# A hybrid transformer layer: the head's convolution from PSUM, wide squares, q's norms by a ones column, decay differences on GpSimd

## The chip, the cores and the metric

The kernel runs on one core of one Trainium2 chip. The metric is the time of one execution in microseconds; each kernel is run three times and the median counts. One further execution is recorded by the hardware profiler, and all rows below come from it. Names of engines: PE is TensorE (matmuls; PEld its weight loads), DVE is VectorE, ACT is ScalarE, POOL is GpSimd, SP is SyncE, which issues the transfers.

## What is computed

One layer on 512 latent and 256 context tokens, 1024 channels wide: a gated feed-forward half step, a mixing step, a second half step, a norm. The mixing step projects the normalised input with one large matrix. Eight heads of 128 channels each take q, k and v from it; this is the part that the change touches. The reference, cut to it:

```python
def short_conv(x, w):                     # 5 taps along the tokens, centred, per channel
    pad = CONV_K // 2
    xp = jnp.pad(x, ((0, 0), (pad, pad), (0, 0)))
    y = sum(xp[:, k:k + L] * w[k] for k in range(CONV_K))
    return jax.nn.silu(y)

def l2norm(x):
    return x * lax.rsqrt(jnp.sum(x * x, axis=-1, keepdims=True) + EPS)
...
    q = l2norm(q) * GDN_HEAD_DIM ** -0.5
    k = l2norm(k)
...
    diff = cum[..., :, None] - cum[..., None, :]      # inside a chunk
    decay = jnp.where(incl, jnp.exp(jnp.where(incl, diff, 0.0)), 0.0)
    lmat = jnp.where(strict, jnp.einsum('nbhid,nbhjd->nbhij', kb, kc) * decay, 0.0)
    sol = lax.linalg.triangular_solve(lmat + eye, rhs, lower=True, unit_diagonal=True)
...
    o = rmsnorm(o.astype(dt), gdn_norm_w) * jax.nn.silu(gate)
```

Every chunk of tokens gives a triangular system, whose inverse feeds a scan over the chunks, once forward and once backward. Context tokens need only k and v.

## The kernel before

Channels lie on the 128 partitions and tokens along the free axis; the kernel works with six chunks of 128 tokens (four latent, two context). Each projection (`job`, L132) is the sum of three matmuls for each of eight slices of the inner dimension, with weights and activations split into a high and a low half; its result for the latent tokens fills one PSUM bank of 512 columns, that for the context tokens (256) another. PSUM has eight banks in three rings: four with tag "b", which the jobs use, two "g" for the scan and two "a" for norms and inversion.

The heads' stage is a software pipeline. `front` makes k's transposed copy kt and the norms of q and k for one head, `invert` builds and inverts the triangular blocks of the head before it, `scan` runs the head before that, and `head` projects and convolves q, k and v of the head three ahead. These are generators; a string of letters gives the order in which their steps are issued, and a list scheduler with its own costs then orders the instructions of each engine. Each engine works through its row in that order.

The steps around the change:

- `conv_silu` (L567 to L587): ACT copies the job's result from PSUM to the padded tile raw (L575, L580), and scales it by the middle tap into cv (L576, L581); DVE adds the four other taps, 772 columns wide for k and v and 512 for q (L583); ACT's silu writes kf, qf or vf (L585, L587). raw and cv exist once each. POOL clears their paddings (L573, L574, L578, L579).
- `front`: k is transposed on PE (L764), ACT copies it to kt (L765) and squares each of the six chunks with an accumulated sum (L768, one read of the accumulator behind each); q is transposed (L771) and squared in the same way (L774). DVE adds epsilon (L776, L777), POOL raises to a power (rr, L780).
- `invert`: rows of cumulated decay come by transfer into crow; ACT makes the absolute difference to each of the twelve columns (arg, L817) and the exponential (L819); DVE multiplies it into L (L827) and into aqk (L836); POOL masks aqk (affine select, L838) and clears ti (L855, L856). ACT copies the diagonal blocks to din (L848), DVE transposes them to au (L850). Then the forward substitution: fifteen steps, each a product tm (L866) and a sum into ti (L868), both on DVE, and two transposes of ti (L870, L872). PE's products that complete the inverse follow (L881 to L926), with copies on ACT and the last products into L on DVE (L930, L934).
- `scan`: for each chunk products on PE (L952, L963, L973, L985, L997), and between them R (L956), vw (L976), S (L994) and ot (L999) on DVE, vn (L980) and scalings on ACT. At its end ACT squares the output in four pieces (L1007), DVE writes y (L1016).
- Weights of the heads' projections are split by ACT (whi, L119) and POOL (wlo, L120); those of the gates by ACT and DVE.

The lines that set this order:

```python
ORDER = "sfifsisiissiis"
for k in range(-2, H):
    stages = {c: g(i) for c, g, i in (("s", scan, k), ("f", front, k + 2), ("i", invert, k + 1)) if 0 <= i < H}
    for c in ORDER:
        if c in stages:
            next(stages[c], None)
```

Of the kernel before, what the change touches and what calls it, by code (L numbers as in the profile page):

```python
# [18 lines left out]
LAT = 512  # L19
# [5 lines left out]
EPS = 1e-6  # L25
# [6 lines left out]
PARTS = {"lat": (0, LAT), "ctx": (LAT, CTX)}  # L32
# [9 lines left out]
def layer_kernel(ctx, tc, a, out):  # L42
    nc = tc.nc
    act, dve, pool, pe, sp = nc.scalar, nc.vector, nc.gpsimd, nc.tensor, nc.sync
# [512 lines left out]
    def bc(ap, shape):  # L557
        return ap.to_broadcast(shape)
# [6 lines left out]
    kf, qf, vf = {}, {}, {}  # L565

    def conv_silu(w, tl, parts, dst, r=None):  # L567
        r = r or job(w, u_hi, u_lo, range(KT), parts)
        raw = pj.tile([128, 776], F32, tag="raw", name="raw", bufs=1)
        cv = pj.tile([128, 772], F32, tag="cv", name="cv", bufs=1)  # L570
        n = 772 if len(parts) == 2 else 512
        tap = [vec[:, 1, 24 * t + tl:24 * t + tl + 1] for t in range(5)]
        pool.memset(raw[:, 0:2], 0.0)  # L573
        pool.memset(raw[:, 514:518], 0.0)  # L574
        act.copy(out=raw[:, 2:514], in_=r["lat"][:, :512])  # L575
        act.activation(out=cv[:, 0:512], in_=r["lat"][:, :512], func=AF.Copy, scale=tap[2])  # L576
        if len(parts) == 2:
            pool.memset(raw[:, 774:776], 0.0)  # L578
            pool.memset(cv[:, 512:516], 0.0)  # L579
            act.copy(out=raw[:, 518:774], in_=r["ctx"][:, :256])  # L580
            act.activation(out=cv[:, 516:772], in_=r["ctx"][:, :256], func=AF.Copy, scale=tap[2])  # L581
# [18 lines left out]
    def col(d, c, h):  # L600
        return d * 48 + c * 8 + h
# [155 lines left out]
    def front(h):  # L757

        kt = mp.tile([128, 6, 128], F32, tag="kt", name="kt", bufs=3)
        ss = mp.tile([128, 10], F32, tag="ss", name="ss", bufs=2)  # L760
        for c0, n in ((0, 4), (4, 2)):
            b = bank("a")
            for c in range(n):
                pe.transpose(b[:, c * 128:(c + 1) * 128], kf[h][:, (c0 + c) * 128:(c0 + c + 1) * 128], ident)  # L764
            act.copy(out=kt[:, c0:c0 + n].rearrange("p c x -> p (c x)"), in_=b[:, :n * 128])  # L765
            for c in range(c0, c0 + n):
                sq = mp.tile([128, 128], F32, tag="sq", name="sq", bufs=2)
                act.activation(out=sq, in_=kt[:, c], func=AF.Square, accum_out=ss[:, c:c + 1])  # L768
        b = bank("a")
        for c in range(4):  # L770
            pe.transpose(b[:, c * 128:(c + 1) * 128], qf[h][:, c * 128:(c + 1) * 128], ident)  # L771
        for c in range(4):
            sq = mp.tile([128, 128], F32, tag="sq", name="sq", bufs=2)
            act.activation(out=sq, in_=b[:, c * 128:(c + 1) * 128], func=AF.Square, accum_out=ss[:, 6 + c:7 + c])  # L774
        nv = mp.tile([128, 10], F32, tag="nv", name="nv", bufs=2)
        dve.tensor_scalar(out=nv[:, 0:6], in0=ss[:, 0:6], scalar1=EPS, scalar2=None, op0=ALU.add)  # L776
        dve.tensor_scalar(out=nv[:, 6:10], in0=ss[:, 6:10], scalar1=EPS, scalar2=128.0, op0=ALU.add, op1=ALU.mult)  # L777

        rr = mp.tile([128, 10], F32, tag="rr", name="rr", bufs=3)
        pool.tensor_tensor(out=rr, in0=nv, in1=powers, op=ALU.pow)  # L780
# [21 lines left out]
    def invert(h):  # L802
# [9 lines left out]
        aqk = mp.tile([128, 8, 128], F32, tag="aqk", name="aqk", bufs=2)  # L812
        arg = mp.tile([128, 2, 6, 128], F32, tag="arg", name="arg", bufs=1)
        for d in range(2):
            for c in range(6):
                q = col(d, c, h)
                act.activation(out=arg[:, d, c], in_=crow[d][:, c], func=AF.Abs, bias=ncumc[:, q:q + 1])  # L817
        af = arg.rearrange("p d c t -> p (d c t)")
        act.activation(out=af, in_=af, func=AF.Exp, scale=-1.0)  # L819
        for c0, n in ((0, 4), (4, 2)):  # L820
# [117 lines left out]
    def scan(h):  # L938
# [329 lines left out]
```

## Time and profile before

| | |
|---|---|
| median of 3 runs | 1750.43 us (1750.38 to 1754.53) |
| the profiled execution | 1756.71 us |
| its span | 1755.0 us |
| granted clock, mean | 0.982 |
| PE busy | 1653.5 us (94%) |
| DVE busy | 1119.0 us (64%) |
| ACT busy | 842.6 us (48%) |
| POOL busy | 390.8 us (22%) |
| chain that ended last | PE 71%, DVE 14%, ACT 5%, DMA 5% |

The span is the profiled execution from its first to its last instruction; the execution's own time lies 1.7 us above. The busy shares are averages over the whole span. The heads' stage, from about 640 to 1240 us, has higher shares of DVE and ACT than the feed-forward steps before and behind it. A timeline row gives start, length, engine, line, operation and tiles, and in brackets the idle time of the engine just before it and what ended it.

### The profile page before, as it was taken

How to read it: one execution, taken by the hardware profiler on the slowest of the kernel's cores; microseconds unless marked ns; L12 is line 12 of the kernel's file. 1: busy time of each engine (PE TensorE's matmuls, PEld its weight loads, DVE VectorE, ACT ScalarE, POOL GpSimd, SP SyncE). 2: the span in 40 equal slices, each digit the busy share in tenths (PEclk: the TensorE clock that was granted, in tenths of full speed). 3: DMA queues.
4: the chain of work that ended last, by engine and by line, in shares of the span. 5: the costliest groups of instructions: out<-in, count | busy, mean ns of one | idle time of the engine just before them, and what ended most of it. 6: DMA issues, size and time to landing. Idle time of an engine off the chain costs nothing.

```text
span 1755.0 us, 31315 instructions
## 1 busy us (share of the span) xinstructions
PE 1653.5 (94%) x12220; PEld 1423.9 (81%) x12220; DVE 1119.0 (64%) x2254; ACT 842.6 (48%) x1851; POOL 390.8 (22%) x493
## 2 busy tenths in 40 slices
PE   6899999999999999889999999999998999999996
PEld 4889898989999778777878788787786788888885
DVE  5778888798888886375678767774555533333333
ACT  5443343434444364667677767665443322222233
POOL 2243444444454121123323331100000000000000
PEclk9999999999999999989999999999999999999998
DMA  9355536361221325532112212224654232333321
GB/s 273 112 155 151 156 96 182 103 189 65 78 67 56 108 82 187 138 100 67 44 52 65 60 45 53 56 61 154 214 158 116 69 98 88 94 96 96 93 64 48
DMA packets 282696, 183.82 MB, mean 105 GB/s; under 512 B 7008, under 2 KB 269877, under 8 KB 282421
## 3 DMA queue, kind: packets, MB, share of 16 engines
q1 hardware_dynamic: 282112, 181.65, 35.6%
q8 instruction: 96, 1.57, 0.4%
q14 instruction: 51, 0.42, 0.1%
q10 hardware_dynamic: 437, 0.18, 0.1%
HBM read 170.22 MB, written 11.58 MB: 104 GB/s over the span
## 4 chain that ended last, share of the span: by engine, by line
PE 71%; DVE 14%; ACT 5%; DMA 5%; POOL 2%; issue 2%; SPq 0%; ACTq 0%; POOLq 0%; DVEq 0%
PE b L132 22%; PE b L345 9%; PE a L132 6%; PE g L132 6%; PE a L345 5%; PE g L345 5%; DVE cv L583 2%; PE b L279 2%; PE a L279 1%; PE g L279 1%; PE a L708 1%; ACT din L848 1%; DVE wlo L120 1%; DMA bg_dram<-bgate 1%; PE b L150 1%
## 5 line engine op out<-in xcount | busy, mean ns | idle before, releaser
L188 ACT CAST fhi<-fst 128x512 fp32r<-128x512 f32 (+1 forms) x136 | 77.7, 605 | 249.6 <-PE b L132 85.6
L132 PE MATMUL b<-hhi,whi 128*128 128x512 f32 (+1 forms) x528 | 187.6, 384 | 0.0
L132 PE MATMUL b<-hlo,whi 128*128 128x512 f32 (+1 forms) x528 | 187.5, 383 | 0.0
L132 PE MATMUL b<-hhi,wlo 128*128 128x512 f32 (+1 forms) x528 | 186.9, 384 | 0.0
L179 POOL TENSOR_TENSOR rs<-rs,mhalf 128x4 f32<-128x4 f32 (+2 forms) x13 | 13.6, 1045 | 665.3 <-DVE rs L177 649.7
L189 DVE TENSOR_TENSOR flo<-fst,fhi 128x512 fp32r<-128x512 f32 (+1 forms) x136 | 87.3, 671 | 92.6 <-ACT fhi L188 92.4
L119 ACT CAST whi<-stg 128x512 fp32r<-128x512 f32 x146 | 89.4, 620 | 91.6 <-PE b L132 59.9
L119 ACT CAST whi<-qst 128x512 fp32r<-128x512 f32 (+1 forms) x160 | 81.6, 512 | 106.5 <-PE b L345 43.2
L119 ACT CAST whi<-qs 128x512 fp32r<-128x512 f32 (+1 forms) x120 | 59.5, 512 | 115.2 <-POOL qs L309 76.2
L583 DVE SCALAR_TENSOR_TENSOR cv<-raw,vec,cv 128x772 f32<-128x772 f32 (+1 forms) x96 | 101.6, 1058 | 11.6 <-ACT cv L581 8.3
L120 DVE TENSOR_TENSOR wlo<-qst,whi 128x512 fp32r<-128x512 f32 (+1 forms) x160 | 100.7, 639 | 10.1 <-ACT whi L119 10.0
L132 PEld LDWEIGHTS b<-hlo,whi 128*128 128x128 f32 x528 | 94.0, 190 | 14.8
L132 PEld LDWEIGHTS b<-hhi,whi 128*128 128x128 f32 x528 | 94.0, 190 | 14.8
L132 PEld LDWEIGHTS b<-hhi,wlo 128*128 128x128 f32 x528 | 93.3, 190 | 14.8
L308 POOL TENSOR_TENSOR qs<-qst 128x512 f32<-128x512 f32 (+1 forms) x40 | 46.4, 1161 | 247.2 <-DMA qst<-in_ffn_w_in_dram 76.6
L120 POOL TENSOR_TENSOR wlo<-stg,whi 128x512 fp32r<-128x512 f32 x46 | 65.4, 1430 | 90.6 <-ACT whi L119 70.6
L120 DVE TENSOR_TENSOR wlo<-stg,whi 128x512 fp32r<-128x512 f32 x100 | 68.2, 686 | 22.1 <-ACT whi L119 20.2
L188 ACT CAST ahi<-q 128x384 fp32r<-128x384 f32 x74 | 37.5, 512 | 75.4 <-DVE q L257 35.6
L120 DVE TENSOR_TENSOR wlo<-qs,whi 128x512 fp32r<-128x512 f32 (+1 forms) x80 | 49.0, 613 | 32.6 <-ACT whi L119 32.6
L132 PE MATMUL b<-xlo,fhi 128*128 128x512 f32 x160 | 63.4, 396 | 0.0
L132 PE MATMUL b<-xhi,flo 128*128 128x512 f32 x160 | 63.4, 396 | 0.0
L132 PE MATMUL b<-xhi,fhi 128*128 128x512 f32 x160 | 63.4, 396 | 0.0
(512 smaller groups left out, 4909.8 us busy)
## 6 DMA issues: line engine op xcount, KB each, us to landing
stg<-in_w_ada_dram SPq DMA_DIRECT2D x56, 512.0 KB, 4.0
stg<-in_w_mix_in_dram SPq DMA_DIRECT2D x49, 512.0 KB, 3.7
fst<-in_ffn_w_in_dram SPq DMA_DIRECT2D x44, 512.0 KB, 3.6
qst<-in_ffn_w_in_dram SPq DMA_DIRECT2D x40, 512.0 KB, 3.4
qst<-in_ffn_w_out_dram SPq DMA_DIRECT2D x40, 256.0 KB, 2.6
adx<-in_w_ada_dram SPq DMA_DIRECT2D x16, 512.0 KB, 6.4
fst<-in_ffn_w_out_dram SPq DMA_DIRECT2D x16, 512.0 KB, 3.9
crow<-cumd SPq DMA_DIRECT2D x16, 384.0 KB, 7.8
```

The lines of the kernel that those rows point to most:

```text
L119: (first.copy if first is act else first.tensor_copy)(out=hi[:, :n], in_=w)
L120: second.tensor_tensor(out=lo[:, :n], in0=w, in1=hi[:, :n], op=ALU.subtract)
L132: pe.matmul(res[p][:, :m], lhsT=ww(i), rhs=hh(k)[:, o:o + m], start=(i == 0 and j == 0), stop=(i == n - 1 and j == 2))
L150: pe.matmul(b[32 * j:32 * j + 32, e * 128:(e + 1) * 128], lhsT=sc[:, k, :], rhs=stg[:, k, :], start=(i == 0), stop=(i == 1))
L188: act.copy(out=hi, in_=src)
L189: dve.tensor_tensor(out=lo, in0=src, in1=hi, op=ALU.subtract)
L279: pe.matmul(x, lhsT=ww(k), rhs=rhs(j, part, k), start=n + e == 0, stop=n + e == len(ks) + 1)
L308: pool.tensor_tensor(out=s1, in0=a21, in1=a22, op=ALU.add)
L345: pe.matmul(o, lhsT=ww[:, k], rhs=rhs(j, part, k), start=first and k + i == 0, stop=k + i == nh + 1, skip_group_check=not first)
L583: dve.scalar_tensor_tensor(out=cv[:, :n], in0=raw[:, t:t + n], scalar=tap[t], in1=cv[:, :n], op0=ALU.mult, op1=ALU.add)
L708: pe.matmul(r[:, :256], lhsT=hh[:, k, t * 128:(t + 1) * 128], rhs=ww[:, k], start=n == 0, stop=n == 3 * KT - 1)
L848: act.copy(out=din[o:o + 32, :, 0:12].rearrange("p f u -> p u f"), in_=L[o:o + 32, :, o:o + 32])
```

## The change

1. Convolution: ACT scales the job's result by the middle tap from PSUM straight into kf, qf or vf; DVE adds the other taps into the same tile, reading the shifted values from PSUM, the latent and the context part apart, each cut at its ends in place of padding; one silu over all columns. raw, cv and the memsets are gone.
2. Squares: kt is squared in one instruction of 768 columns, and DVE sums it by chunks; the output is squared in one instruction of 512, summed on DVE, and multiplied by the square of q's norm factor (two products of four columns) to stand for the scale that the old squares had.
3. q's norms: qf is squared untransposed, and four matmuls with a column of ones sum it over the partitions.
4. Decay differences: POOL adds the cumulated columns to crow, 768 wide, for each direction; ACT takes the absolute value, 768 wide.

```diff
-        raw = pj.tile([128, 776], F32, tag="raw", name="raw", bufs=1)
-        cv = pj.tile([128, 772], F32, tag="cv", name="cv", bufs=1)
...
-        act.copy(out=raw[:, 2:514], in_=r["lat"][:, :512])
-        act.activation(out=cv[:, 0:512], in_=r["lat"][:, :512], func=AF.Copy, scale=tap[2])
...
+        spans = [(r[p], *PARTS[p]) for p in parts]
+        for x, o, n in spans:
+            act.activation(out=dst[:, o:o + n], in_=x[:, :n], func=AF.Copy, scale=tap[2])
         for t in (0, 1, 3, 4):
-            dve.scalar_tensor_tensor(out=cv[:, :n], in0=raw[:, t:t + n], scalar=tap[t], in1=cv[:, :n],
-                                     op0=ALU.mult, op1=ALU.add)
-        act.activation(out=dst[:, 0:512], in_=cv[:, 0:512], func=AF.Silu)
-        if len(parts) == 2:
-            act.activation(out=dst[:, 512:768], in_=cv[:, 516:772], func=AF.Silu)
+            for x, o, n in spans:
+                i0, i1 = max(0, 2 - t), n - max(0, t - 2)
+                d = dst[:, o + i0:o + i1]
+                dve.scalar_tensor_tensor(out=d, in0=x[:, i0 + t - 2:i1 + t - 2], scalar=tap[t], in1=d, op0=ALU.mult, op1=ALU.add)
+        n = sum(PARTS[p][1] for p in parts)
+        act.activation(out=dst[:, :n], in_=dst[:, :n], func=AF.Silu)
...
-            for c in range(c0, c0 + n):
-                sq = mp.tile([128, 128], F32, tag="sq", name="sq", bufs=2)
-                act.activation(out=sq, in_=kt[:, c], func=AF.Square, accum_out=ss[:, c:c + 1])
+        sq = mp.tile([128, 6, 128], F32, tag="sq", name="sq", bufs=1)
+        act.activation(out=sq, in_=kt, func=AF.Square)
+        dve.tensor_reduce(out=ss, in_=sq, axis=AX.X, op=ALU.add)
+        sq = mp.tile([128, LAT], F32, tag="sqq", name="sqq", bufs=1)
+        act.activation(out=sq, in_=qf[h], func=AF.Square)
         b = bank("a")
         for c in range(4):
-            pe.transpose(b[:, c * 128:(c + 1) * 128], qf[h][:, c * 128:(c + 1) * 128], ident)
-        for c in range(4):
-            sq = mp.tile([128, 128], F32, tag="sq", name="sq", bufs=2)
-            act.activation(out=sq, in_=b[:, c * 128:(c + 1) * 128], func=AF.Square, accum_out=ss[:, 6 + c:7 + c])
+            pe.matmul(b[:, c:c + 1], lhsT=sq[:, c * 128:(c + 1) * 128], rhs=ones[:, 0:1])
...
-            for c in range(6):
-                q = col(d, c, h)
-                act.activation(out=arg[:, d, c], in_=crow[d][:, c], func=AF.Abs, bias=ncumc[:, q:q + 1])
+            own = ncumc.rearrange("p (d c h) -> p d c h", d=2, c=6)[:, d, :, h:h + 1]
+            pool.tensor_tensor(out=arg[:, d], in0=crow[d], in1=bc(own, [128, 6, 128]), op=ALU.add)
+            act.activation(out=arg[:, d], in_=arg[:, d], func=AF.Abs)
...
-        for c in range(4):
-            act.activation(out=sq[:, c], in_=ot[:, c], func=AF.Square, scale=rr[:, 6 + c:7 + c], accum_out=so[:, c:c + 1])
+        act.activation(out=sq, in_=ot, func=AF.Square)
+        dve.tensor_reduce(out=so, in_=sq, axis=AX.X, op=ALU.add)
+        dve.tensor_tensor(out=s2, in0=rr[:, 6:10], in1=rr[:, 6:10], op=ALU.mult)
+        dve.tensor_tensor(out=so, in0=so, in1=s2, op=ALU.mult)
```

The scheduler orders the whole stage anew. Three places show what stands where; a number behind a tile's name tells its copies apart, and "x2" stands for two in a row.

DVE at the end of the second head's inversion, before: L930 and L934 are its last products, L583 the taps of v, L976 the scan's vw.

```order
L1016 SCALAR_TENSOR_TENSOR y<-g,vec,sgate 128x512
L934 TENSOR_TENSOR L<-TN,bs 64x6x64 x2
L930 TENSOR_TENSOR L<-a,bs 64x6x64
L583 SCALAR_TENSOR_TENSOR cv<-raw,vec,cv 128x772 x4
L976 TENSOR_TENSOR vw<-g,w_8134 128x256
L956 SCALAR_TENSOR_TENSOR R<-g,necum,vt 128x128 x2
L776 TENSOR_SCALAR nv<-ss 128x6
```

The same place with the change, where the taps are L578, the products L922 and L926, and vw L968.

```order
L1010 SCALAR_TENSOR_TENSOR y<-g,vec,sgate 128x512
L926 TENSOR_TENSOR L<-TN,bs 64x6x64
L578 SCALAR_TENSOR_TENSOR vf<-b,vec,vf 128x254
L926 TENSOR_TENSOR L<-TN,bs 64x6x64
L578 SCALAR_TENSOR_TENSOR vf<-b,vec,vf 128x511
L578 SCALAR_TENSOR_TENSOR vf<-b,vec,vf 128x255
L578 SCALAR_TENSOR_TENSOR vf<-b,vec,vf 128x511
L578 SCALAR_TENSOR_TENSOR vf<-b,vec,vf 128x255
L922 TENSOR_TENSOR L<-a,bs 64x6x64
L578 SCALAR_TENSOR_TENSOR vf<-b,vec,vf 128x510
L578 SCALAR_TENSOR_TENSOR vf<-b,vec,vf 128x254
L968 TENSOR_TENSOR vw<-g,w_8074 128x256
```

Six of v's eight taps now stand ahead of the last product into L, two behind it and ahead of vw.

POOL at the start of the second head's forward substitution, before: L838 masks aqk, L855 and L856 clear ti.

```order
L840 MEMSET L 64x6x64
L855 MEMSET ti 128x1056
L120 TENSOR_TENSOR wlo<-stg,whi 128x512
L856 MEMSET ti 128x32
L838 AFFINE_SELECT aqk<-aqk 128x512 x2
L120 TENSOR_TENSOR wlo<-stg,whi 128x512
L789 COPY w_9664<-bwst 128x6
```

The same place with the change: L830 masks aqk, L847 and L848 clear ti, L808 are the new adds for the next head.

```order
L832 MEMSET L 64x6x64
L830 AFFINE_SELECT aqk<-aqk 128x512
L847 MEMSET ti 128x1056
L830 AFFINE_SELECT aqk<-aqk 128x512
L848 MEMSET ti 128x32
L808 TENSOR_TENSOR arg<-crow,ncumc 128x768 x2
L120 TENSOR_TENSOR wlo<-stg,whi 128x512
L781 COPY w_9529<-bwst 128x6
```

The two adds have come in between the clearing of ti with the masks and the split of the next weights.

DVE from the transpose into au (L850) at the start of the same forward substitution, before.

```order
L850 STREAM_TRANSPOSE au<-din 128x1024
L994 TENSOR_TENSOR S<-S,g 128x256
L836 TENSOR_TENSOR aqk<-a,arg 128x512 x2
L956 SCALAR_TENSOR_TENSOR R<-g,necum,vt 128x128 x2
L866 TENSOR_TENSOR tm<-au,ti 128x30
L868 TENSOR_TENSOR ti<-ti,tm 128x2x15
L866 TENSOR_TENSOR tm<-au,ti 128x56
L868 TENSOR_TENSOR ti<-ti,tm 128x2x14x2
L866 TENSOR_TENSOR tm<-au,ti 128x78
L976 TENSOR_TENSOR vw<-g,w_7957 128x256
L868 TENSOR_TENSOR ti<-ti,tm 128x2x13x3
```

The same stretch with the change: au is L842, the substitution's product and sum are L858 and L860, the taps of k L578.

```order
L828 TENSOR_TENSOR aqk<-a,arg 128x512
L842 STREAM_TRANSPOSE au<-din 128x1024
L986 TENSOR_TENSOR S<-S,g 128x256
L858 TENSOR_TENSOR tm<-au,ti 128x30
L860 TENSOR_TENSOR ti<-ti,tm 128x2x15
L858 TENSOR_TENSOR tm<-au,ti 128x56
L860 TENSOR_TENSOR ti<-ti,tm 128x2x14x2
L948 SCALAR_TENSOR_TENSOR R<-g,necum,vt 128x128 x2
L858 TENSOR_TENSOR tm<-au,ti 128x78
L860 TENSOR_TENSOR ti<-ti,tm 128x2x13x3
L578 SCALAR_TENSOR_TENSOR kf<-b,vec,kf 128x510
L968 TENSOR_TENSOR vw<-g,w_7912 128x256
```

The products with the decay (aqk) now stand ahead of the transpose, R behind the second step of the substitution, and the first tap of k comes within its first three steps.

## Rows read from the trace of the kernel before

**Rows 1.** Stretches: us, then busy us (instructions) by engine, PEclk, DMA, GB/s
```profile
core 0: us, PE busy (x) PEld busy (x) DVE busy (x) ACT busy (x) POOL busy (x), PEclk, DMA share, GB/s
816.75:840.30 23.55, 21.53 (x136) 18.05 (x134) 22.44 (x60) 19.70 (x50) 5.22 (x8) 1.00 0.26 57
840.30:876.70 36.40, 34.61 (x539) 29.36 (x540) 23.08 (x44) 23.69 (x65) 15.38 (x27) 1.00 0.18 52
876.70:900.60 23.90, 22.39 (x136) 18.82 (x135) 22.38 (x58) 18.26 (x45) 4.11 (x8) 1.00 0.30 78
900.60:932.60 32.00, 30.84 (x518) 26.18 (x519) 18.22 (x40) 24.34 (x69) 13.55 (x25) 1.00 0.15 43
```

**Rows 2.** Timeline of DVE, 850 to 868 us: start, length, what, idle before
```profile
857.33 0.56 DVE L930 TENSOR_TENSOR L<-a,bs 64x384 f32<-64x384 f32 x1 [4.66 <-PE a L926]
...
857.92 6.61 DVE L583 SCALAR_TENSOR_TENSOR cv<-raw,vec,cv 128x772 f32<-128x772 f32 x4
...
864.56 0.42 DVE L976 TENSOR_TENSOR vw<-g,w 128x256 f32<-128x256 f32 x1
```

**Rows 3.** Timeline of PE, 862.5 to 868 us
```profile
865.04 0.71 PE L985 MATMUL g<-vw,kt 128*128 128x128 f32 x4 [1.78 <-DVE vw L976]
```

**Rows 4.** Chain of waits, 800 to 960 us: start, length, engine, line
```profile
866.30 1.17 ACT sq L768 x8
...
867.93 0.70 ACT sq L768 x4
```

**Rows 5.** Groups of instructions by shape, ACT: busy us, mean ns, idle before
```profile
L575 ACT COPY raw<-b 128x512 f32<-128x512 f32 x24 | 13.9, 579 | 0.1
...
L580 ACT COPY raw<-b 128x256 f32<-128x256 f32 x16 | 6.0, 372 | 0.0
...
L768 ACT ACTIVATE sq<-kt 128x128 f32<-128x128 f32 x48 | 14.2, 306 | 0.0
...
L768 ACT ACTIVATION_READ_ACCUMULATOR sq<-kt 128x1 f32 x48 | 9.4, 196 | 0.0
...
L817 ACT ACTIVATE arg<-crow,ncumc 128x128 f32<-128x128 f32 x96 | 30.8, 398 | 7.0 <-DMA crow<-cumd 7.0
```

**Rows 6.** Groups of instructions by shape, DVE
```profile
L583 DVE SCALAR_TENSOR_TENSOR cv<-raw,vec,cv 128x772 f32<-128x772 f32 x64 | 76.4, 1194 | 9.1 <-ACT cv L581 8.3 <-issue 0.3
...
L1016 DVE SCALAR_TENSOR_TENSOR y<-g,vec,sgate 128x512 f32<-128x512 f32 x8 | 6.0, 751 | 21.1 <-PE g L1014 21.1
...
L437 DVE SCALAR_TENSOR_TENSOR xT<-g,eff,xT 128x384 f32<-128x384 f32 x20 | 12.1, 607 | 0.0
```

**Rows 7.** Timeline of DVE, 873 to 885 and 932.6 to 956 us
```profile
878.56 0.19 DVE L866 TENSOR_TENSOR tm<-au,ti 128x30 f32<-128x30 f32 x1
...
932.68 1.25 DVE L850 STREAM_TRANSPOSE au<-din 128x1024 f32<-128x1024 f32 x1 [1.89 <-ACT din L848]
...
941.60 1.31 DVE L866 TENSOR_TENSOR tm<-au,ti 128x128 f32<-128x128 f32 x1
...
942.94 0.29 DVE L868 TENSOR_TENSOR ti<-ti,tm 128x128 f32<-128x128 f32 x1
...
950.30 1.02 DVE L583 SCALAR_TENSOR_TENSOR cv<-raw,vec,cv 128x772 f32<-128x772 f32 x1
```

**Rows 8.** Timeline of POOL, 850 to 885 and 925 to 960 us
```profile
877.74 0.17 POOL L856 MEMSET ti<- 128x32 f32 x1
...
927.42 1.99 POOL L780 TENSOR_TENSOR rr<-nv,powers 128x10 f32<-128x10 f32 x1
...
941.47 1.28 POOL L120 TENSOR_TENSOR wlo<-stg,whi 128x512 fp32r<-128x512 f32 x1 [5.29 <-PE b L132]
```

**Rows 9.** One line's durations, min, median, max in ns: L827
```profile
L827 DVE SCALAR_TENSOR_TENSOR L<-a,nbs,arg x96: 309/342/352, 752.2 to 1150.6; 128x128 f32<-128x128 f32 x96
```

**Rows 10.** Timeline of ACT, 847 to 882 us
```profile
880.99 0.36 ACT L980 ACTIVATE vn<-g,bs 128x128 f32<-128x128 f32 x1
```

**Rows 11.** Chain of waits, PE's matmuls, 827 to 830 us
```profile
827.19 1.87 PE b L132 x8
...
829.05 0.44 PE g L985 x4
```

More of the change, by code (lines that the diff above doesn't have):

```diff
@@ L568, in conv_silu @@
         r = r or job(w, u_hi, u_lo, range(KT), parts)
-        raw = pj.tile([128, 776], F32, tag="raw", name="raw", bufs=1)
-        cv = pj.tile([128, 772], F32, tag="cv", name="cv", bufs=1)
-        n = 772 if len(parts) == 2 else 512
         tap = [vec[:, 1, 24 * t + tl:24 * t + tl + 1] for t in range(5)]
-        pool.memset(raw[:, 0:2], 0.0)
-        pool.memset(raw[:, 514:518], 0.0)
-        act.copy(out=raw[:, 2:514], in_=r["lat"][:, :512])
-        act.activation(out=cv[:, 0:512], in_=r["lat"][:, :512], func=AF.Copy, scale=tap[2])
-        if len(parts) == 2:
[L578 to L581, printed above, removed]
-        for t in (0, 1, 3, 4):
-            dve.scalar_tensor_tensor(out=cv[:, :n], in0=raw[:, t:t + n], scalar=tap[t], in1=cv[:, :n],
-                                     op0=ALU.mult, op1=ALU.add)
-        act.activation(out=dst[:, 0:512], in_=cv[:, 0:512], func=AF.Silu)
-        if len(parts) == 2:
-            act.activation(out=dst[:, 512:768], in_=cv[:, 516:772], func=AF.Silu)
+        spans = [(r[p], *PARTS[p]) for p in parts]
+        for x, o, n in spans:
+            act.activation(out=dst[:, o:o + n], in_=x[:, :n], func=AF.Copy, scale=tap[2])
+        for t in (0, 1, 3, 4):
+            for x, o, n in spans:
[4 more added lines that the diff above has]
+        act.activation(out=dst[:, :n], in_=dst[:, :n], func=AF.Silu)
     def head(h):
@@ L759, in front @@
         kt = mp.tile([128, 6, 128], F32, tag="kt", name="kt", bufs=3)
-        ss = mp.tile([128, 10], F32, tag="ss", name="ss", bufs=2)
+        ss = mp.tile([128, 6], F32, tag="ss", name="ss", bufs=2)
         for c0, n in ((0, 4), (4, 2)):
@@ L765, in front @@
             act.copy(out=kt[:, c0:c0 + n].rearrange("p c x -> p (c x)"), in_=b[:, :n * 128])
-            for c in range(c0, c0 + n):
-                sq = mp.tile([128, 128], F32, tag="sq", name="sq", bufs=2)
-                act.activation(out=sq, in_=kt[:, c], func=AF.Square, accum_out=ss[:, c:c + 1])
+        sq = mp.tile([128, 6, 128], F32, tag="sq", name="sq", bufs=1)
[3 more added lines that the diff above has]
+        act.activation(out=sq, in_=qf[h], func=AF.Square)
         b = bank("a")
         for c in range(4):
-            pe.transpose(b[:, c * 128:(c + 1) * 128], qf[h][:, c * 128:(c + 1) * 128], ident)
-        for c in range(4):
-            sq = mp.tile([128, 128], F32, tag="sq", name="sq", bufs=2)
-            act.activation(out=sq, in_=b[:, c * 128:(c + 1) * 128], func=AF.Square, accum_out=ss[:, 6 + c:7 + c])
+            pe.matmul(b[:, c:c + 1], lhsT=sq[:, c * 128:(c + 1) * 128], rhs=ones[:, 0:1])
         nv = mp.tile([128, 10], F32, tag="nv", name="nv", bufs=2)
-        dve.tensor_scalar(out=nv[:, 0:6], in0=ss[:, 0:6], scalar1=EPS, scalar2=None, op0=ALU.add)
-        dve.tensor_scalar(out=nv[:, 6:10], in0=ss[:, 6:10], scalar1=EPS, scalar2=128.0, op0=ALU.add, op1=ALU.mult)
+        dve.tensor_scalar(out=nv[:, 0:6], in0=ss, scalar1=EPS, scalar2=None, op0=ALU.add)
+        dve.tensor_scalar(out=nv[:, 6:10], in0=b[:, 0:4], scalar1=EPS, scalar2=128.0, op0=ALU.add, op1=ALU.mult)
         rr = mp.tile([128, 10], F32, tag="rr", name="rr", bufs=3)
@@ L1002, in scan @@
             yield
-        so = mp.tile([128, 4], F32, tag="so", name="so", bufs=1)
+        so, s2 = (mp.tile([128, 4], F32, tag=n, name=n, bufs=1) for n in ("so", "so2"))
         sq = mp.tile([128, 4, 128], F32, tag="yo", name="sqo", bufs=1)
-        for c in range(4):
-            act.activation(out=sq[:, c], in_=ot[:, c], func=AF.Square, scale=rr[:, 6 + c:7 + c], accum_out=so[:, c:c + 1])
+        act.activation(out=sq, in_=ot, func=AF.Square)
+        dve.tensor_reduce(out=so, in_=sq, axis=AX.X, op=ALU.add)
+        dve.tensor_tensor(out=s2, in0=rr[:, 6:10], in1=rr[:, 6:10], op=ALU.mult)
+        dve.tensor_tensor(out=so, in0=so, in1=s2, op=ALU.mult)
         r = rstd_of(so, 4, 128)
```

## The prediction

> **What bounds the kernel now.** I read the busy shares by engine first, then the chain of waits over the heads' stage, then a table of stretches, and only then single instructions. The change touches nothing outside the heads' stage, which in this trace lasts from about 640 to 1240 us; its steady part, where one head is scanned while the next is inverted and a third is projected, repeats every 58 us. One such iteration has two stretches of different character, shown for two iterations in [rows 1]: one where DVE substitutes forward (from the transpose into au at L850 to the second transpose at L872) and the rest. In the forward substitution DVE is busy 22.44 of 23.55 us and 22.38 of 23.90: DVE sets its length. In the rest PE is busy 34.61 of 36.40 and 30.84 of 32.00, DVE only 23.08 and 18.22: PE sets it. So the most that any edit can gain by shortening waits is PE's idle time. In the rest that is 1.79 and 1.16 us, 1.5 an iteration; in the substitution 2.02 and 1.51, 1.8 an iteration. Some 370 of the stage's 600 us are such iterations (the others fill and empty the pipeline), 6.4 of them, so the caps are 9.4 us in the rest and 11.3 in the substitution, together 20.7 of 1750.
>
> The rest's idle time has two visible causes. [Rows 2]: after a gap of 4.66 us DVE runs v's four taps in one piece, 6.61 us, and only then vw. [Rows 3]: PE stands 1.78 us for that vw. The taps could not use the gap because the one raw tile and the one cv tile were still q's. The other is ACT: [rows 4] shows squares and their accumulator reads of k and q as pieces of the chain, 1.17 + 0.70 us in one iteration.
>
> **The change part by part.** The sum is made as a difference. The profiled execution took 1756.7 us (span 1755.0), the median of the runs is 1750.43; I apply the difference to the median. About 0.3%, 5 us, is what a measurement of this kernel can tell from no change.
>
> *Convolution.* For k and for v ACT loses the two copies out of PSUM (0.579 + 0.372, [rows 5]), for q one; that is 13.9 + 6.0 us over eight heads, and the silu comes in one piece. DVE did four taps of 1.194 mean [rows 6], that is 4.78 a job, and now does eight, four of 512 and four of 256, from PSUM. A tap of 512 with an operand in PSUM costs 0.751 (the y row), one of 384 costs 0.607, so by the same slope one of 256 costs 0.46: 4 x (0.75 + 0.46) = 4.84. Bounds: 0 against the mean; against an old tap that met nothing (1.02, [rows 7]) 0.8 more a job, for six k jobs in the substitution 4.6 us. I take 0, since the mean is what the old taps cost in fact. With raw and cv gone, six of v's eight taps stand in the gap ahead of the last product of the inversion, two behind it: 2.4 in place of 6.6 us, of which 1.2 ahead of vw. The 1.78 us wait of PE goes. What is late next there is vw's own matmul on PE. The memsets on POOL that go cost nothing today.
>
> *Squares.* k's six squares with their reads (14.2 + 9.4 us over eight heads, [rows 5]) become one of 768 wide, at most the 0.95 of a 512 and a 256 copy together: 7.6. The twelve pieces of arg (30.8) become two Abs of 768: 15.2. With copies, q's and the output's squares ACT loses about 70 us over the stage. ACT bounds no stretch of [rows 1] (19.70 of 23.55 us at most, 84%), so this is worth only what of it PE waited for. DVE gains a reduction of 768 and one of 512 and two tiny products a head, at 0.75 to 1.2 us for the wide one about 2.4 a head, in the rest, where DVE has 13 us spare: 0, or 2.4 a head, 15 over the iterations, if that cover were gone. q's four transposes become four matmuls of one column: 0, PE's other work hides them.
>
> So in the rest I let PE's whole idle time go: **-9.4 us**; ends 0 and -20.7.
>
> *Decay differences on POOL.* This is the term that decides. The two adds of 768 a head read two tiles in SBUF. Nothing in the trace is an add of that shape; POOL's subtraction of 512, also of two tiles in SBUF, takes 1.28 us [rows 8], so an add of 768 is an estimated 1.9. In POOL's new order both stand behind the memsets of ti (directly in four of the seven iterations, in three behind the second select of aqk, which comes about then too), and the last of these memsets is what the substitution's first product waits for. So both start when the substitution starts. What then happens is in [rows 7]: tm's product takes 0.19 to 0.28 us by itself, and 1.31 when it meets POOL's subtraction that started 0.13 us before it [rows 8]. DVE is held until POOL is done. That it is a matter of operands, [rows 9] show: the products at L827, with one input in PSUM, never took more than 0.352 us, and POOL's power that makes rr, 1.99 us of two SBUF tiles [rows 8], runs among them in each iteration. The substitution's thirty operations have both inputs in SBUF. Placed into the iteration at 877 us: POOL is free at 877.91 [rows 8], the first add would run to 879.8, the first product, due at 878.56 [rows 7], waits 1.26 us; while it runs the second add is queued and takes the next turn, and the second product waits some 1.85 us: 3.1 us together, where DVE sets the length of the stretch. Of this I let 0.5 vanish in the 1.1 to 1.5 us that DVE idles in such a stretch. It happens in seven substitutions (the last head has no next one): 7 x 2.6 = **+18.2 us**. Ends: 0, if POOL runs the adds under DVE's transpose or its PSUM operations, and 7 x 3.8 = 26.7. The Abs behind them on ACT stand just ahead of vn; the first add ends at 879.8 and vn went at 880.99 [rows 10], so that wait is nil.
>
> The Trainium skill ("SBUF — State Buffer", Who interferes with whom) says that a DVE instruction with two SBUF inputs and a GpSimd instruction that reads SBUF exclude each other for the whole instruction, and that one with a single SBUF input is free. The trace agrees (1.31 against 0.28; 0.352 at most). Taken to the letter each add would cost its whole length, and the sum would be 1768.
>
> *Banks.* The four "b" banks were free after ACT's copy; now the last tap frees them. From the end of k's job to v's context matmul PE has q's 24 matmuls at 0.234, 5.6 us, and some eight pairs of scan matmuls at 0.44, 3.5 us [rows 11], 9.1 in all; DVE has k's taps (4.8), twelve operations of the substitution at 0.28 (3.4) and about five scan steps of vw's kind at 0.42 (2.1), 10.3 in all. So the bank comes about 1.2 us late, twice an iteration in six iterations: up to 14 us. The substitution's PE idle time covers most of it: I take 0, ends 0 and 14.
>
> Sum: 1750.4 - 9.4 + 18.2 = **1759**.
>
> **The rivals.** *A, the adds cost little (not slower).* Place: the start of the substitution. If DVE gets its turn between the adds, or POOL finishes them while DVE still waits for din, the loss is under 1.3 us a head, and from there down the gain in the rest wins: at nil 1750.4 - 9.4 = 1741. For it: DVE idled up to 1.89 us for din ahead of au [rows 7], time in which an add that comes early is free. Against it: in POOL's new order they stand behind the memset that the first product needs. *B, a wash.* Half of the lock's price: 7 x 1.3 = 9.1 against 9.4, 1750. *C, banks too.* The 14 us come on top: 1773; decided by whether PE stands for a tap ahead of v's context matmuls. The Trainium skill ("PSUM — Partial Sum Buffer", Summary: rules for kernel authors) says "Evacuate promptly"; no trace here shows a bank held by taps. *D, everything gains.* No lock, and the substitution loses its PE idle time too: 1750.4 - 20.7 = 1730. Against it: DVE fills that stretch and loses nothing.
>
> **How the numbers follow.** Forecast 1759 (1753 to 1766): 0.37. A: 0.25. B: 0.22. C: 0.08. D: 0.08. Faster by over 0.3% is A and D, 0.33; within is B, 0.22; slower the forecast and C, 0.45. The range leaves out D below and C above, 0.16, and takes in A's 1741 with the 4 us by which its gain may be mis-sized: 1737 to 1771. The forecast's own range is 1753 to 1766.
>
> **What would show it.** In the profile after: the two adds of about 1.9 us right behind ti's memset, and the first products of the substitution at over 1 us in place of 0.2; the substitution 26 to 27 us long in place of 23.7. The rest with PE idle under 0.5 us, vw no longer waited for. ACT down by about 70 us. Taps from PSUM at 0.75 and 0.46, whatever POOL does. It is wrong if the first products stay at 0.2 to 0.3 (then A), if PE's idle time in the rest stays at 1.5 us, or if PE waits for taps ahead of v's context matmuls (then C).

## The result, and the profile after

The changed kernel takes 1762.33 us (1759.03 to 1764.03, 5 runs) against 1754.52 us of the kernel before in the same comparison: a ratio of 1.0055, 95% interval 1.004 to 1.007. By the ratio it is slower by 9.6 us (0.55% of 1754.5); the two medians lie 7.8 us apart, and the two profiled executions (1756.71 and 1762.33 us) 5.6. The forecast was 1759, 8.8 us over the median of 1750.4 that it started from.

The page of the kernel after, engines' busy time, share and instructions:

```profile
PE 1657.2 (94%) x12252; PEld 1432.5 (81%) x12252; DVE 1142.3 (65%) x2350; ACT 793.2 (45%) x1515; POOL 399.0 (23%) x429
```

ACT has 49 us less than before (842.6), DVE 23 more (1119.0). The stretches that answer to [rows 1], the second and third substitution and the rest behind each (columns as there):

```profile
814.20:841.50 27.30, 24.02 (x151) 21.07 (x150) 25.21 (x65) 15.37 (x31) 5.82 (x7) 0.94 0.21 49
841.50:872.60 31.10, 30.91 (x518) 26.29 (x519) 19.62 (x47) 20.93 (x41) 13.68 (x19) 1.00 0.22 62
872.60:902.40 29.80, 25.71 (x155) 22.11 (x153) 27.25 (x68) 15.70 (x32) 5.53 (x6) 0.94 0.18 45
902.40:933.70 31.30, 31.08 (x520) 26.32 (x520) 21.42 (x49) 21.03 (x41) 13.80 (x19) 1.00 0.22 61
```

The rest has hardly any idle time of PE left: 0.19 and 0.22 us, where [rows 1] had 1.79 and 1.16. The substitutions are longer, 27.3 and 29.8 us for 23.6 and 23.9, and PE idles 3.28 and 4.09 us in them for 2.02 and 1.51. The reason stands at the start of each. DVE at the second substitution (timeline: start, length, what, idle before):

```profile
815.79 1.43 DVE L858 TENSOR_TENSOR tm<-au,ti 128x30 f32<-128x30 f32 x1
817.25 1.42 DVE L860 TENSOR_TENSOR ti<-ti,tm 128x30 f32<-128x30 f32 x1
818.71 1.19 DVE L858 TENSOR_TENSOR tm<-au,ti 128x56 f32<-128x56 f32 x1
819.94 0.22 DVE L860 TENSOR_TENSOR ti<-ti,tm 128x56 f32<-128x56 f32 x1
820.07 0.60 DVE L948 SCALAR_TENSOR_TENSOR R<-g,necum,vt 128x128 f32<-128x128 f32 x2
```

POOL at the same time:

```profile
815.60 0.16 POOL L848 MEMSET ti<- 128x32 f32 x1
815.68 2.93 POOL L808 TENSOR_TENSOR arg<-crow,ncumc 128x768 f32<-128x768 f32 x2
818.55 1.28 POOL L120 TENSOR_TENSOR wlo<-stg,whi 128x512 fp32r<-128x512 f32 x1
```

And PE:

```profile
820.73 1.22 PE L965 MATMUL g<-R,L 128*128 128x128 f32 x4 [3.05 <-DVE R L948]
```

POOL finishes clearing ti and starts the two adds; the first product of the substitution, 0.19 us in [rows 7], takes 1.43, the sum behind it 1.42, and the next product meets POOL's split of weights and takes 1.19. Each ends with the POOL operation beside it. R, which reads PSUM and one SBUF tile, is queued behind them, although the product that it reads left PE at 816.65 us, and PE stands 3.05 us for R. PE's waits from 750 to 1240 us (what waited, for whom, us in total, times, longest):

```profile
PE g L965 <- DVE R L948: 14.1, 6, 4.4
PE b L132 <- ACT whi L119: 2.6, 1, 2.6
PE a L873 <- DVE tr L864: 2.2, 6, 0.5
PE g L977 <- ACT vn L973: 1.6, 1, 1.6
...
PE g L977 <- DVE vw L968: 0.8, 1, 0.8
```

The same view of the kernel before, from 752 us on:

```profile
PE g L952 <- DVE S L994: 5.1, 6, 1.2
...
PE g L985 <- DVE vw L976: 3.8, 2, 2.0
...
PE a L824 <- ACT sq L774: 1.1, 2, 0.6
...
PE g L973 <- DVE R L956: 0.6, 1, 0.6
```

The wait for R is the loss, 14.1 us for 0.6 (the one for S, which stands just ahead of R in the scan, fell from 5.1 to 1.0). The one for vw, 1.78 us in [rows 3] and 3.8 in all, is there once with 0.8 us. No wait of PE for a tap is in the list.

### The profile page after: what moved, and what is told of

Same layout as the page of the kernel before. It is cut to its first block, busy times and chain, and to the rows that moved or that the text cites. A ratio compares the mean times of both kernels' runs of the same rounds, so it can differ in the third digit from the quotient of the medians.

```text
span 1760.6 us, 31012 instructions
## 1 busy us (share of the span) xinstructions
PE 1657.2 (94%) x12252; PEld 1432.5 (81%) x12252; DVE 1142.3 (65%) x2350; ACT 793.2 (45%) x1515; POOL 399.0 (23%) x429
## 4 chain that ended last, share of the span: by engine, by line
PE 73%; DVE 14%; ACT 3%; DMA 3%; issue 3%; POOL 2%; SPq 0%; ACTq 0%; POOLq 0%; DVEq 0%
PE b L132 25%; PE b L345 8%; PE g L132 6%; PE a L132 6%; PE a L345 5%; PE g L345 5%; PE b L279 2%; DVE wlo L120 1%; PE a L279 1%; PE a L701 1%; DVE xT L437 1%; PE g L279 1%; PE g L965 1%; PE b L150 1%; DVE tm L858 1%
## 5 line engine op out<-in xcount | busy, mean ns | idle before, releaser
L132 PE MATMUL b<-hhi,wlo 128*128 128x512 f32 (+1 forms) x528 | 190.6, 390 | 0.0
L120 DVE TENSOR_TENSOR wlo<-qst,whi 128x512 fp32r<-128x512 f32 (+1 forms) x160 | 104.8, 664 | 10.2 <-ACT whi L119 10.1
L120 POOL TENSOR_TENSOR wlo<-stg,whi 128x512 fp32r<-128x512 f32 x46 | 59.1, 1289 | 98.1 <-ACT whi L119 82.8
L120 DVE TENSOR_TENSOR wlo<-qs,whi 128x512 fp32r<-128x512 f32 (+1 forms) x80 | 48.6, 607 | 27.3 <-ACT whi L119 25.5
L437 DVE SCALAR_TENSOR_TENSOR xT<-q,eff,xT 128x128 f32<-128x128 f32 (+2 forms) x100 | 63.0, 651 | 0.1
```

The costliest lines, as they stand in the source:

```text
L120: second.tensor_tensor(out=lo[:, :n], in0=w, in1=hi[:, :n], op=ALU.subtract)
L437: dve.scalar_tensor_tensor(out=r[:, o0:o1], in0=c[i][j][:, o0 - j * n2:o1 - j * n2], scalar=gate(m + i, s), in1=r[:, o0:o1], op0=ALU.mult, ...
```

## The experiments

All orders of the stage but those of the last two runs differ from the order of the kernel they are held against, since the scheduler plans anew at each edit. So a second measure stands beside the time, read from each run's trace over the stage, from the first scaling of the convolution to the last y: the sum of the 240 operations of the eight substitutions, PE's idle time, and the work that PE lost at the lower clock (the sum over stretches of 2 us of 2 us times one less the granted clock). In the kernels before and after, and in runs 1, 3, 4, 11 and 12, the stage's length less the last two is 544 to 546 us, so these two account for its differences; in the other runs it is 539 to 550.

| kernel | ratio to before (95%) | substitutions | PE idle | lost to clock |
|---|---|---|---|---|
| before | 1 | 64.4 | 33.9 | 6.8 |
| after | 1.0055 (1.004 to 1.007) | 78.8 | 34.9 | 11.9 |
| 1: differences on ACT | 0.9955 (0.994 to 0.9969) | 65.0 | 20.0 | 8.5 |
| 2: only the adds | 1.0194 (1.0168 to 1.022) | 74.2 | 48.9 | 29.0 |
| 3: memsets for adds | 0.9955 (0.994 to 0.997) | 62.8 | 20.1 | 10.2 |
| 4: adds behind TN | 1.0113 (1.0093 to 1.0132) | 60.6 | 21.8 | 35.8 |
| 5: only convolution | 1.0038 (1.0019 to 1.0057) | 65.7 | 31.9 | 17.1 |
| 6: only squares, norms | 1.0035 (1.0021 to 1.0049) | 63.7 | 31.2 | 13.6 |
| 7: two raw, two cv | 1.0126 (1.0103 to 1.0149) | 67.5 | 46.5 | 20.5 |
| 8: adds behind the transpose | 1.014 (1.0117 to 1.0162) | 63.7 | 34.9 | 34.1 |
| 9: before, one sq tile | 1.0095 (1.0074 to 1.0116) | 65.4 | 34.1 | 15.4 |
| 10: 1, and split on DVE | 1.0011 (0.9998 to 1.0025) | 60.0 | 27.7 | 18.8 |
| 11: copies, same order | 0.9979 (0.9966 to 0.9992) | 69.9 | 23.8 | 10.2 |
| 12: scalar adds, same order | 1.0006 (0.9991 to 1.0021) | 69.9 | 27.6 | 10.2 |

**1. The adds undone.** The changed kernel with ACT's twelve differences again:

```diff
-            own = ncumc.rearrange("p (d c h) -> p d c h", d=2, c=6)[:, d, :, h:h + 1]
-            pool.tensor_tensor(out=arg[:, d], in0=crow[d], in1=bc(own, [128, 6, 128]), op=ALU.add)
-            act.activation(out=arg[:, d], in_=arg[:, d], func=AF.Abs)
+            for c in range(6):
+                q = col(d, c, h)
+                act.activation(out=arg[:, d, c], in_=crow[d][:, c], func=AF.Abs, bias=ncumc[:, q:q + 1])
```

> The changed kernel with only its fourth part undone: ACT makes the twelve absolute differences with a bias again, POOL adds nothing. Theory (the adds hold DVE at the start of the forward substitution): the thirty operations of a substitution fall from 78.9 us over eight heads to about 65, PE's waits for R in the product of the scan (14.1 us) go, and of the gain in the rest most stays though ACT has 15 us more: 1748 us (1744 to 1752). Rival (the substitution is longer because k's and q's taps from PSUM now stand in it, eight and up to three a head): 1758 to 1763, the products of the substitution as short as in the theory but the stretch still 26 to 28 us.

1744.57 us, 17.8 under the changed kernel and faster than both. The substitutions fell to 65.0, PE's idle time by 15. The waits that answer to those above, from 740 to 1240 us:

```profile
PE a L766 <- ACT kt L758: 6.8, 1, 6.8
...
PE g L977 <- DVE vw L968: 2.4, 3, 0.9
PE g L965 <- DVE R L948: 2.2, 3, 1.0
```

R costs 2.2 us in place of 14.1. The rival is out: the taps from PSUM stand in the substitution here too, and two of the long ones still last 26 us, with PE idle for 1.3 and 2.1 us in them.

**2. The adds alone.** The reverse edit in the kernel before.

> The kernel before with only the fourth part done: POOL adds, two wide absolute values on ACT. Convolution, squares and norms as before. Theory: the substitution's operations rise by 12 to 16 us over eight heads, and nothing is gained elsewhere, since v's taps still stand in one piece ahead of vw: 1764 us (1758 to 1770). Rival (the loss comes from the convolution): within 4 us of the kernel before, 1750 to 1756.

1785.01 us against 1752.97: 32 us slower, over twice what was expected. The substitutions rose by 9.8 us, less than forecast; PE's idle time rose by 15 and the work lost to the clock by 22. So the adds hold the substitution without the other parts too. How much of the 32 us is theirs and how much the new order's, this run does not show.

**3. POOL as long busy, but reading nothing.** Two memsets for each add:

```diff
-            pool.tensor_tensor(out=arg[:, d], in0=crow[d], in1=bc(own, [128, 6, 128]), op=ALU.add)
-            act.activation(out=arg[:, d], in_=arg[:, d], func=AF.Abs)
+            pool.memset(arg[:, d], 0.0)
+            pool.memset(arg[:, d], 0.0)
+            act.activation(out=arg[:, d], in_=crow[d], func=AF.Abs)
```

> The changed kernel with each add of 1.49 us replaced by two memsets of the same tile (about 0.74 us each, from the memset of TN of the same width), which read nothing; ACT takes the absolute value of crow without the cumulated column, so the decay is left out in part. POOL is as long busy at the same place. Theory (it is POOL's reading of SBUF that holds DVE): the first products stay at 0.2 to 0.3 us, 1746 us (1742 to 1751). Rival (POOL's row is simply longer, so that the clearing of ti and the masks come late): 1757 to 1763.

1745.73 us, as expected. POOL at the third substitution (timeline):

```profile
873.33 0.17 POOL L848 MEMSET ti<- 128x32 f32 x1
873.39 1.43 POOL L807 MEMSET arg<- 128x768 f32 x2
874.75 1.42 POOL L808 MEMSET arg<- 128x768 f32 x2
```

DVE beside it:

```profile
873.53 0.20 DVE L858 TENSOR_TENSOR tm<-au,ti 128x30 f32<-128x30 f32 x1 [2.17 <-POOL ti L848]
873.77 0.21 DVE L860 TENSOR_TENSOR ti<-ti,tm 128x30 f32<-128x30 f32 x1
874.02 0.22 DVE L858 TENSOR_TENSOR tm<-au,ti 128x56 f32<-128x56 f32 x1
874.27 0.22 DVE L860 TENSOR_TENSOR ti<-ti,tm 128x56 f32<-128x56 f32 x1
```

POOL is busy for 2.8 us beside the same products, and they take 0.20 to 0.22 us. The clearing of ti does come late here, DVE idles 2.17 us for it, as the rival has it; the kernel is 16.6 us under the changed one all the same. It is not that POOL works, it is that it reads SBUF.

**4 and 8. The adds moved out of the substitution.** In both the changed kernel's adds wait, by a copy of one column into arg, for a tile of the head before: TN in run 4, the last transpose in run 8.

```diff
+            if last_tn:
+                pool.tensor_copy(out=arg[:, d, 0, 0:1], in_=last_tn[-1][:, 0, 0:1])
             pool.tensor_tensor(out=arg[:, d], in0=crow[d], in1=bc(own, [128, 6, 128]), op=ALU.add)
```

> The changed kernel with the adds of a head made to wait for TN of the head before, by a copy of one column into arg ahead of each: they then stand behind the substitution, in the stretch where PE sets the time and most of DVE's operations read PSUM. Theory: the substitution is free of them and ACT stays light: 1745 us (1739 to 1750), faster than both kernels. Rival (the adds cost their time wherever they meet DVE): 1756 to 1762.

> The changed kernel with the adds made to wait for the last transpose of the substitution of the head before (a copy of one of its columns into arg ahead of each), so some 5 us earlier than when they waited for TN. Theory (the late adds lost by the clock that fell to half for 13 us an iteration while PE ran small products with little else between them, not by meeting DVE; here PE has more of the projection between these products): no substitution operation over 1 us, clock near 1.00, 1744 us (1738 to 1750). Rival (the adds cost as much behind the substitution, or the clock falls here too): 1756 to 1772.

1772.42 and 1779.7 us: both expectations missed, and both rivals' ranges too. The half on the substitution held in sum (60.6 and 63.7 us), though in run 8 single products still took up to 1.22 us. In run 4 PE's idle time was 21.8, nearly as low as in run 1: what was lost is clock. Run 8 lost nearly as much clock, and 14.9 us of idle time more than run 1 besides, 3.0 of it in two waits for taps of v. Run 4 behind its third substitution (columns of [rows 1]):

```profile
900.00:904.00 4.00, 4.00 (x181) 3.46 (x174) 3.80 (x10) 1.28 (x4) 2.82 (x5) 1.00 0.02 4
904.00:908.00 4.00, 2.82 (x94) 2.33 (x98) 3.47 (x7) 3.34 (x7) 1.08 (x1) 0.91 0.17 66
908.00:912.00 4.00, 4.00 (x90) 3.07 (x80) 1.11 (x3) 2.21 (x5) 1.42 (x3) 0.50 0.66 172
912.00:916.00 4.00, 4.00 (x20) 2.96 (x21) 0.00 (x0) 2.34 (x4) 2.15 (x2) 0.50 0.51 138
916.00:920.00 4.00, 4.00 (x25) 3.50 (x22) 0.00 (x0) 2.27 (x4) 1.29 (x3) 0.50 0.55 140
```

PE's granted clock is half (1.2 GHz) for 13.7 us here, behind a stretch in which the order gave PE the small products of the inversion with little of the projection between them, and a wait. It is so in five iterations, for 10 to 14 us each. Whether adds at that place would be free in another order stays open.

**5, 6, 7 and 9. Single parts, and a new order by itself.** Run 5 is the kernel before with the new `conv_silu` alone, run 6 with the new squares and norms alone, both as in the diff above. Run 7 gives the kernel before two raw and two cv tiles, and one sq tile for room; run 9 only the latter:

```diff
-        raw = pj.tile([128, 776], F32, tag="raw", name="raw", bufs=1)
-        cv = pj.tile([128, 772], F32, tag="cv", name="cv", bufs=1)
+        raw = pj.tile([128, 776], F32, tag="raw", name="raw", bufs=2)
+        cv = pj.tile([128, 772], F32, tag="cv", name="cv", bufs=2)
...
-                sq = mp.tile([128, 128], F32, tag="sq", name="sq", bufs=2)
+                sq = mp.tile([128, 128], F32, tag="sq", name="sq", bufs=1)
```

> The kernel before with only the first part: convolution from PSUM into its result; squares, norms and decay as before. Theory (v's late taps cost PE's idle time ahead of vw, and taps from PSUM cost DVE as much as the old ones): PE's wait for vw goes, 1747 us (1743 to 1751). Rival (eight taps in the substitution, where DVE sets the time, cost up to 0.8 us a job and the four banks come free late): 1755 to 1765, with PE waiting for taps in its row of waits.

> The kernel before with only the second and third part: wide squares with sums on DVE, q's norms by a ones column; convolution and decay as before. Theory (ACT's squares stood in the chain of the rest, 1.9 us in one iteration): 1748 us (1744 to 1752). Rival (ACT's time was worth nothing, PE sets the rest anyway, or the sums on DVE cost as much): 1752 to 1757.

> The kernel before with two raw and two cv tiles (and one sq tile in place of two, for room), all else as it was. It tests the claim that the single tiles kept v's taps behind the last product into L. Theory: q's and v's taps overlap, PE's wait of 1.8 us for vw shrinks, 1746 us (1743 to 1750). Rival (in DVE's new row v's four taps of 772 still stand in one piece ahead of vw, so it was the length and place of the taps and not the buffer): 1750 to 1756.

> The kernel before with one sq tile in place of two, which takes no work away and adds none; ACT writes all of them in its own order anyway. The scheduler orders the stage anew (748 lines of DVE's row differ). It measures what a new order alone is worth, and is what the run with two raw tiles is to be held against. Theory (the verdicts on single parts, 8 us slower each, lie within what a new order does): it moves by 5 us or more either way, 1745 to 1775. Rival (the order is worth little, and these verdicts are the parts' own): 1750 to 1756.

1760.59, 1760.53, 1777.02 and 1767.43 us: the expectations of runs 5, 6 and 7 were missed, that of run 9 was met. The time of run 5 is its rival's; those of runs 6 and 7 lie above their rivals' too. Run 9 takes no work away and adds none, and is slower by 0.95%: a new order alone is worth more than runs 5 and 6 lost (0.38 and 0.35%), and most of what run 7 lost, which has run 9's edit in it. So the verdicts of runs 5 to 7 can't be put down to their parts. The same goes for the 0.55% of the change as a whole; only runs 11 and 12 keep an order. What their traces say is narrower. Run 5 has one wait of PE for a tap, 1.0 us. Run 6 keeps the wait for vw in the rest (5.6 us in four places). Run 5 has none for vw there; its waits for S and vw (3.7 and 2.9) lie in the substitutions, and in the rest PE waits 5.6 us for ot, which ACT scales. In run 7 v's four taps still stand in one piece ahead of vw in DVE's row in three iterations (two in the kernel before), although there are two tiles of each.

**10. The split of the heads' weights on DVE,** on top of run 1 (`EH = (act, dve)`).

> The changed kernel with ACT making the absolute differences (as in the first run) and, in addition, DVE in place of POOL splitting the weights of the heads (46 subtractions, about 0.69 us each on DVE, 1.29 on POOL). The last reads of two SBUF tiles by POOL inside the substitution are gone. Theory: no substitution operation over 0.7 us, sum about 60 us, but DVE gets some 31 us of work, four to six subtractions an iteration, of which those inside the substitution lengthen it: 1746 us (1741 to 1752), no better than the first run's 1744.6. Rival (every read of POOL in SBUF costs more than it brings): 1738 to 1742.

1756.04 us, over the range: no operation of the substitution is over 0.7 us any more (60.0 in sum), and the kernel is 11 us slower than run 1. PE idles 7.7 us more and loses 10 more to the clock. Of the two, the forecast had only the first.

**11 and 12. The same order, another operation.** Two edits leave every engine's row as it is in the changed kernel, instruction for instruction; only POOL's operation at L808 is another.

```diff
-            pool.tensor_tensor(out=arg[:, d], in0=crow[d], in1=bc(own, [128, 6, 128]), op=ALU.add)
+            pool.tensor_copy(out=arg[:, d], in_=crow[d])
```

```diff
+            pool.tensor_scalar(out=arg[:, d], in0=crow[d], scalar1=ncumc[:, 0:1], scalar2=None, op0=ALU.add)
```

> The changed kernel with POOL copying crow into arg in place of adding, so the cumulated column is left out of the decay: one tile read in place of two. The order of every engine's row is the same as in the changed kernel, instruction for instruction, so no new order comes in. Theory (the adds' hold on DVE sets the loss): if the copy is shorter than the add's 1.49 us, say 0.75 to 1.0, the substitution's operations fall from 78.8 us to 68 to 73 and the time by 5 to 12 us, to 1750 to 1757 against the changed kernel's 1762; if it takes as long, nothing moves. Rival (the loss lies in the order that the scheduler found): 1760 to 1764 whatever the copy takes.

> The changed kernel with POOL adding one column for all six chunks as a scalar operand in place of a tile of columns, so the decay is wrong in five of six chunks: again one tile read, and again every engine's row in the order of the changed kernel. A second point for the copy's run. Theory: the time moves with the operation's length, down by about as much as the substitution's operations lose in sum and up to 1.5 times that where PE's clock stays up too: 1750 to 1758 if the operation takes about 1 us. Rival: 1760 to 1764 whatever it takes.

The copy takes 0.84 us (median) where the add took 1.49, and the time falls to 1750.02, 12.3 us under the changed kernel, at the long end of what was expected; the substitutions lose 8.9 us, PE's idle time 11.1, the work lost to the clock 1.7. PE's wait for R, 14.1 us with the adds, is about half (750 to 1240 us):

```profile
PE g L965 <- DVE R L948: 7.4, 5, 3.1
```

This is the cleanest of the runs: with the order held, the time falls as POOL's reads hold DVE for less.

The scalar add was a surprise: it takes 2.22 us, longer than the add, and yet the substitutions sum to 69.9 as with the copy, and the time is 1755.6, under the changed kernel and not over it. That the time moves with the operation's length, as was expected, is not so. Run 12, POOL at the second substitution (timeline):

```profile
811.64 4.45 POOL L808 TENSOR_SCALAR arg<-crow,ncumc 128x768 f32<-128x768 f32 x2
```

DVE beside it:

```profile
811.74 0.86 DVE L858 TENSOR_TENSOR tm<-au,ti 128x30 f32<-128x30 f32 x1
812.63 0.22 DVE L860 TENSOR_TENSOR ti<-ti,tm 128x30 f32<-128x30 f32 x1
812.88 0.22 DVE L858 TENSOR_TENSOR tm<-au,ti 128x56 f32<-128x56 f32 x1
...
814.05 0.82 DVE L860 TENSOR_TENSOR ti<-ti,tm 128x78 f32<-128x78 f32 x1
```

The first product is held, the next ones are not, and one is held again when the second operation starts: POOL holds DVE for some 0.7 us at the start of each of the two and lets it go while it is still busy; the other substitutions of the run show the same. What the run loses against the copy, 5.6 us, is elsewhere: PE waits less for R (3.5 us for 7.4), but 6.0 us for vn (0.2 with the copy), which ACT makes behind the absolute values that wait for POOL (PE's waits, 750 to 1240 us):

```profile
PE g L965 <- DVE R L948: 3.5, 3, 2.7
PE g L989 <- ACT vn L972: 3.3, 3, 1.6
PE g L977 <- ACT vn L973: 2.7, 1, 2.7
```

## Why the prediction was right, point by point

**What bounds each stretch** held: the substitution by DVE, the rest by PE, and their sum the time.

**The rest, -9.4 us.** The direction was right and the size was over. From the second to the last substitution PE's idle time in the rest ahead of each fell from 7.6 to 2.0 us (runs' traces, the seven gaps summed): 5.6 us. The term was taken as 1.5 us an iteration from two iterations; the seven had 0.1 to 2.1. The two causes that were named are gone from the rest: the waits for vw (3.8 us) and for q's squares (1.1). Which part of the change took each away is argued and not shown, since runs 5 and 6 are orders of their own; that run 5 has no wait for vw in the rest and run 6 keeps it speaks for the convolution.

**The adds, +18.2 us.** The mechanism was right in place, order and operands; runs 1, 3 and 11 show it from three sides. The size was over, and it came by another way. An add takes 1.49 us and not 1.9, so that two take 2.9; the operations of the substitutions rose by 14.4 us over seven heads, 2.1 each for the 2.6 taken. Only part of that is seen as PE's idle time in the eight substitutions, 13.03 us before and 22.46 after: +9.4. Another part was not in the sum at all: behind three waits of PE for R the granted clock is half (1.2 GHz) for some 3.4 us. After the wait of 3.05 us shown above and after that at 881 us:

```profile
820.00:824.00 4.00, 3.27 (x11) 2.80 (x12) 3.71 (x12) 1.53 (x4) 0.00 (x0) 0.57 0.58 136
...
880.00:884.50 4.50, 3.43 (x11) 2.86 (x12) 4.17 (x13) 2.14 (x4) 0.14 (x1) 0.68 0.52 114
```

Over the stage PE loses 5.1 us more to the lower clock than before.

**The sum.** One more term was not in it: ahead of the first substitution and behind the last one PE idles 2.8 us less than before (its wait for the first kt alone fell from 9.0 to 6.7). So the traces give 9.4 + 5.1 = 14.5 us of loss for the 18.2 taken, and 5.6 + 2.8 = 8.4 of gain for the 9.4 taken: 6.1 us, where the two profiled executions differ by 5.6. The times of runs 1 and 3, in orders of their own, give like sizes: 8.4 and 7.2 us under the kernel before without the adds, 17.8 and 16.6 under the changed kernel. Both terms were too large, in opposite directions, and two that were left out, the clock and the stage's ends, pulled in opposite directions too. That the forecast came within 4 us is in part luck.

**The path from DVE to PE.** The prediction argued by the length of the substitution and let the delay end at its end. The trace shows it earlier: PE waits for R (14.1 us in six places), which needs nothing from POOL and only stands behind the held operations in DVE's row.

**Convolution, 0.** Taps of 510 and 511 columns from PSUM take 0.735 to 0.744 us on average and those of 254 and 255 0.474, whatever POOL does:

```profile
L578 DVE SCALAR_TENSOR_TENSOR kf<-b,vec,kf 128x510 f32<-128x510 f32 x16 | 11.9, 744 | 3.5 <-ACT kf L573 3.5
...
L578 DVE SCALAR_TENSOR_TENSOR kf<-b,vec,kf 128x254 f32<-128x254 f32 x16 | 7.6, 474 | 0.0
```

0.75 and 0.46 were taken. The working's "2.4 in place of 6.6 us" for v's late taps counts four taps where the order has two behind the last product; these took 1.14 us ahead of vw in one iteration of the trace after (at 859.69 us). But the reason given for v's late taps, the single raw and cv tiles, is not borne out: with two of each the scheduler left them where they were (run 7).

**Squares, 0 on the path.** DVE's sums cost 0.946 us for 768 and 0.668 for 512, within what was taken. ACT lost 49 us and not 70: the groups' sums of [rows 5] count a square and the read of its sum in full, 0.306 + 0.196 us, but on the engine they overlap: eight of them, four pairs, took 1.17 us in [rows 4], 0.29 a pair. The wide pieces cost what was taken or less (0.85 us for 768 columns).

**Banks, 0.** No wait of PE for a tap on a "b" bank in the trace after: rival C is out. In other runs there were some: one of 1.0 us in run 5, two of 3.0 together in run 8, under 0.7 in five more, far from the 14 that C asked for. The Trainium skill's "Evacuate promptly" ("PSUM — Partial Sum Buffer", Summary: rules for kernel authors) found no case in the changed kernel, with banks held for four or eight taps, and small ones in other runs.

**The wait of the absolute values, nil.** ACT did wait for the adds, 12.1 us in eight places, but PE only 1.6 us for vn behind them; with a slower operation (run 12) it became 6.0.

**The Trainium skill's rule** ("SBUF — State Buffer", Who interferes with whom) named the right pairs of operations: run 3 and the trace after agree (0.20 us beside memsets, 1.43 beside adds). That the hold lasts for the whole instruction is so for the add and the split, and not for the scalar add of run 12.

## What to carry to other kernels

Before work goes to GpSimd, look at what VectorE runs at that moment: operations with both inputs in SBUF waited here for GpSimd's reads (1.43 us in place of 0.19), and everything behind them in VectorE's row waited along, also what reads PSUM. Judge a part of a change by the wait that it adds or removes in the trace and by runs that keep the order: where a scheduler plans anew, the new plan alone moved this kernel by 0.95%. The version to keep is the changed kernel with the differences left on ScalarE (0.9955 of the kernel before).

## What the hardware showed that was not expected

In the changed kernel each of three waits of PE for R, of 3.05 to 4.42 us, was followed by half the clock for some 3.4 us, so that it cost about half as much again. A GpSimd scalar add of 768 columns took 2.22 us against 1.49 of an add of two tiles and 0.84 of a copy, yet held VectorE no longer than the copy did (69.9 us of substitutions with either). Memsets on GpSimd that took as long as the adds (2.85 us for 2.93) did not hold it.
